# Hybrid decoder layer on one core: other figures in the model of engine times that orders the program, and four gate blocks in place of two ahead of the SSM's drain

## The chip, the cores and the metric

The kernel runs on one core of a Trainium2 chip. The metric is the device time of one execution in microseconds (us), median of several. Engines are named as in the profile: PE (TensorE, matrix multiply), PEld (its weight loads), DVE (VectorE), ACT (ScalarE), POOL (GpSimd) and SP (SyncE, which here only issues transfers). Each works off its own queue of instructions in order and waits on semaphores of the others.

## What is computed

One decoder layer on 512 tokens of width 1024, in float32. Cut to what matters here:

```python
h = rms_norm(x, norm_mix)
qa, ka, va, u, qm, km, vm, gates = split_in(h @ w_in)
oa = swa_attention(qa, ka, va, sinks, slopes)       # window of 128
ys = s5_ssm(u, ...)            # 32 groups: B u, complex scan over time, Re(C h) + D u
z  = gelu(ys) @ w_glu
yb = (z[:, :512] * sigmoid(z[:, 512:])) @ w_o_ssm
om = moba_attention(qm, km, vm, slopes)              # blocks of 256
g  = sigmoid(gates)                                   # 3 x 1024 columns
x  = x + (g0 * (oa @ w_o_swa) + g1 * yb + g2 * (om @ w_o_moba)) @ w_out
x  = x + square(relu(rms_norm(x, norm_ffn) @ w_ff1)) @ w_ff2
out = rms_norm(x, norm_final)
```

## The kernel before, in words

**Dense blocks.** The projections are cut into blocks of 128 output columns. `dense()` computes one: for each of 8 slices of the contraction three matmuls (high part of the weight by high and by low part of the input, low part of the weight by high part), so 24 matmuls of 128x512 into one of two PSUM banks with the tag `acc`. The weights come through `Stream`: SP loads `wraw`, ACT rounds it (`w<-wraw`, CAST) and DVE subtracts for the low part (`w<-wraw,w`); these two are emitted some half blocks ahead of their use. After a block, its bank is emptied: for a gate by one ACT instruction (`gb<-acc`); for a query block `q` by two of ACT and two of DVE (`q<-acc`); for the key block `k` by two chains ACT, ACT, DVE, ACT, one for each half. Block n+2 can't start before block n's bank is empty.

**The plan.** `plan` lists the blocks in order: 4 of the SSM's input `u`, 8 gates of branch 0, SWA's 4 `q`, `k` and `v`, then A gates, the SSM's drain, the start of SWA attention, MoBA's 4 `q`, `k`, `v`, then B gates, SWA's drain, the start of MoBA attention, C gates, and the output projections. Gates of branches 1 and 2 are taken in order from one list, so A, B and C only say where the next ones stand.

**Side work.** The SSM and both attentions are generators, woven between the matmuls of dense blocks: after each slice `dense()` calls `step()`, which lets a side generator emit its next piece when its inputs are ready. "Ready" is not measured: while the program is built, every call of an engine goes through `Engine`, which adds an estimated cost to that engine's clock `clk` and notes when each tile is written. `step()` compares those clocks, and takes nothing more when ACT's or DVE's clock is past the end that is passed in. A `drain` emits what is left of a branch with no dense block between.

```python
def step(end, most=4):
    for _ in range(most):
        if max(clk["ACT"], clk["DVE"]) > end + SLACK:
            return
        x = next((x for x in sides if x.ready() <= clk["PE"] + 0.1), None)
        if x is None:
            return
        x.run()
```

**The SSM's side work.** First `ssm_b`, `ssm_c` and `ssm_phasors` build tables: transposes `pz` evacuated by ACT to `zl`, ACT's pads `ca`, small products `pg`, cosines and sines. Then `ssm_run` treats four groups in two generators, two groups each, one tile `own` for each generator. A group is: products `er`, `ei` on PE (PSUM tag S, three banks); six DVE products and sums and two scans into `own` (called stage 1 below); six more DVE instructions through tiles `p`, `t` into `own` (stage 2); 12 products `y` on PE; then ACT square, two of DVE, ACT tanh and one of DVE into `U`. The drain ends with 16 transfers `yt<-U` on POOL's queue.

**Attention.** A unit has its scores `s` on PE (tag S too), DVE's biased maximum (`p<-s`, `mx`), ACT's exponentials, DVE's scaling, and for each block of keys transposes `pt`, a rounding `th` on ACT, the rest `tl` on DVE, and two products `po`; at the end ACT's `ot` and DVE's `raw` free the one bank of `po` for the next unit.

Of the kernel before, what the change touches and what calls it, by code (L numbers as in the profile page):

```python
# [19 lines left out]
def trunk(ctx: ExitStack, tc: tile.TileContext, x, norm_mix, w_in, sinks, lam_re, lam_im,  # L20
# [3 lines left out]
    clk = dict.fromkeys(("PE", "ACT", "DVE", "POOL", "DMA"), 0.0)  # L24
# [17 lines left out]
    def on_chip(v):  # L42
        return isinstance(v, bass.AP) and not v.tensor.name.startswith(("in_", "out_"))

    def account(eng, outs, ins, cost, after=0.0):
        t = max([clk[eng], ready(*ins) if ins else 0.0])
        for o in outs:
            t = max(t, free_at.get(o.tensor.name, 0.0),
                    max(touched.get(c, 0.0) for c in cells(o)))
        clk[eng] = t + cost  # L50
        for o in outs:
            for c in cells(o):
                written[c] = t + cost + after
        for v in outs + ins:
            for c in cells(v):
                touched[c] = max(touched.get(c, 0.0), t + cost + after)
# [14 lines left out]
    class Engine:  # L71
# [6 lines left out]
        def __getattr__(self, op):  # L78
            f = getattr(self.e, op)

            def call(o, *a, **k):
                outs = [v for v in (o, k.get("accum_out")) if v is not None and on_chip(v)]
                ins = [v for v in list(a) + list(k.values()) if on_chip(v) and
                       v is not k.get("accum_out")]
                n = 1
                for d in o.shape[1:]:
                    n *= d
                if op == "dma_start":
                    account("DMA", outs, ins, max(0.5, n * o.shape[0] * 1.1e-5), 1.5)
                    return f(o, *a, **k)  # L90
                if self.name == "PE":
                    if op == "transpose":
                        cost = 0.109
                    elif a[0].dtype == F32R:
                        cost = max(n, 256) * 4.24e-4
                    else:
                        cost = max(n, 32) * 1.68e-3
                elif self.name == "ACT":
                    aps = sum(on_chip(v) for v in k.values())
                    cost = 0.06 + n * 8.3e-4 + 0.093 * aps  # L100
                elif self.name == "DVE":
                    if op == "tensor_tensor_reduce":
                        outs.append(a[-1])
                        n += 60
                    cost = 0.07 + n * (5.2e-4 if op in ("tensor_scalar", "tensor_copy") else
                                       1.04e-3)
                else:
                    cost = 0.1 + n * 1.75e-3
                account(self.name, outs, ins, cost)
                return f(o, *a, **k)  # L110

            return call

    PE, ACT, DVE, POOL, SP = (Engine(e, n) for e, n in (
        (nc.tensor, "PE"), (nc.scalar, "ACT"), (nc.vector, "DVE"), (nc.gpsimd, "POOL"),
        (nc.sync, "SP")))
# [25 lines left out]
    def PS(tag, name, shape=(128, 512)):  # L142
        b = {"acc": 2, "S": 3, "T": 2, "O": 1}[tag]
        return slot(tag, b, psum.tile(list(shape), F32, tag=tag, name=nm_(name), bufs=b))
# [79 lines left out]
    plan += [("g", 0, m) for m in range(8)]  # L224
    plan += [("q", "swa", m) for m in range(4)] + [("k", "swa"), ("v", "swa")]
    gs_ = [("g", 1, m) for m in range(8)] + [("g", 2, m) for m in range(8)]
    A, B, C, D, E = 2, 8, 2, 1, 1

    def some(n):
        return [gs_.pop(0) for _ in range(min(n, len(gs_)))]  # L230
# [22 lines left out]
    for job in plan:  # L253
        if job[0] in where:
            w, k, c, width = where[job[0]]
# [376 lines left out]
# [8 lines that stand above are left out]
# [5 lines left out]
    def dense(xh, xl, nk=8):  # L645

        acc = PS("acc", "acc")
        for k in range(nk):
            if k % 4 == 0:
                w = ws.take()  # L650
            rh, rl = xh(k), xl(k)
            PE.matmul(acc, w[:, 0, k % 4, :], rh, start=(k == 0), stop=False)
            PE.matmul(acc, w[:, 0, k % 4, :], rl, start=False, stop=False)
            PE.matmul(acc, w[:, 1, k % 4, :], rh, start=False, stop=(k == nk - 1))
            step(clk["PE"] + (nk - 1 - k) * 0.64)
        return acc

    h_h = lambda k: hh[k // 4][:, k % 4, :]
# [194 lines left out]
    def proj_q(b, pair):  # L853
        d = BR[b]
        acc = dense(h_h, h_l)
        g, e = pair // 2, (pair % 2) * 2
        if g not in d["q"]:
            d["q"][g] = B8([128, 4, 512], "q", F32R)
        q = d["q"][g]
        lo, hi = slice(0, 64), slice(64, 128)  # L860
        s0, s1 = (0.125 / slopes[(8 if b == "moba" else 0) + 2 * pair + i] for i in range(2))
        ACT.mul(q[lo, e, :], acc[lo], s0)
        ACT.mul(q[hi, e + 1, :], acc[hi], s1)
        stt(q[hi, e, :], acc[lo], s0, q[lo, e, :].bitcast(F32), MUL, SUB)
        stt(q[lo, e + 1, :], acc[hi], s1, q[hi, e + 1, :].bitcast(F32), MUL, SUB)

    def proj_k(b):
        d = BR[b]
        acc = dense(h_h, h_l)
        K = d["k"] = B8([128, 2, 2, 512], "k", F32R)  # L870
        for g in range(2):
            p, o = slice(64 * g, 64 * g + 64), slice(64 - 64 * g, 128 - 64 * g)
            ACT.copy(K[p, 0, g, :], acc[p])
            ACT.copy(K[o, 0, g, :], acc[p])
            tt(K[p, 1, g, :], acc[p], K[p, 0, g, :].bitcast(F32), SUB)
            ACT.copy(K[o, 1, g, :], K[p, 1, g, :].bitcast(F32))

    def proj_v(b):
        d = BR[b]
        acc = dense(h_h, h_l)  # L880
        vt = B2([128, 512], "vt")
        ACT.copy(vt, acc)
        d["vt"] = vt
# [820 lines left out]
```

## Time and profile before

| | |
|---|---|
| median of 3 runs | 798.91 us (796.45 to 800.1) |
| the profiled execution | 798.28 us, of which the span from the first to the last instruction 796.5 us |
| granted TensorE clock, mean | 0.995 |
| PE busy | 773.5 us, 97% of the span |
| DVE, ACT busy | 589.5 us (74%), 440.7 us (55%) |
| PE in the chain that ended last | 81% of the span |

Busy time of PE holds overlap: matmuls are pipelined, so a record is longer than the distance to the next one. Waits of PE are what the sections below look for. Dense blocks run from the start to about 417 us; behind them the last projection, the two products of the feed-forward part and the final norm follow.

### The profile page before, as it was taken

Reading aid. Unit: us, or ns where it says so; the run is one execution under the profiler, and the core shown is the slowest. Engines: PE = TensorE matmul, PEld = TensorE weight load, DVE = VectorE, ACT = ScalarE, POOL = GpSimd, SP = SyncE. Lnnn points to the kernel's source line nnn. Section 1 sums busy time; section 2 is a strip of 40 time slices with the busy share of each in tenths; the row PEclk is TensorE's granted clock in tenths of the full one; section 3 lists DMA queues with packets and bytes.
Section 4 is the critical chain, followed back from the end, with each engine's and each line's share of the span. In section 5 each row is a group of like instructions: output and inputs, shape, how many; then the busy total and the mean of one; then the engine's idle time right before and its main releaser. Section 6 shows DMA issues by size and latency. Waiting matters only on the chain.

```text
span 796.5 us, 11554 instructions
## 1 busy us (share of the span) xinstructions
PE 773.5 (97%) x4234; PEld 662.5 (83%) x4234; DVE 589.5 (74%) x1176; ACT 440.7 (55%) x848; POOL 92.0 (12%) x140
## 2 busy tenths in 40 slices
PE   7999999989999999999999999999999999999996
PEld 6887778778888887888888888899999888888885
DVE  5885698766796588877575536888888598976774
ACT  7586733464775566653244425666666565655623
POOL 6041020040011222002212132000000000000000
PEclk9999999999999999999999999999999999999998
DMA  9352373253335789429999899733133565555702
GB/s 244 109 155 77 120 205 94 74 125 118 94 112 158 177 214 257 110 85 301 315 348 262 160 205 259 199 110 103 49 86 96 196 241 185 196 175 173 249 1 105
DMA packets 117720, 130.28 MB, mean 164 GB/s; under 512 B 5304, under 2 KB 87264, under 8 KB 117664
## 3 DMA queue, kind: packets, MB, share of 16 engines
q1 hardware_dynamic: 102544, 91.26, 37.3%
q0 software_dynamic: 14928, 38.03, 20.8%
q8 instruction: 33, 0.54, 0.3%
q10 hardware_dynamic: 192, 0.27, 0.1%
q14 instruction: 23, 0.19, 0.1%
HBM read 119.30 MB, written 37.49 MB: 197 GB/s over the span
## 4 chain that ended last, share of the span: by engine, by line
PE 81%; DVE 12%; ACT 3%; issue 2%; DMA 1%; SPq 0%; DVEq 0%; ACTq 0%
PE f L110 40%; PE acc L110 27%; PE xo L110 5%; DVE w L110 4%; DVE own L110 2%; PE s L110 2%; PE po L110 2%; PE pt L110 2%; PE y L110 1%; DVE t L110 1%; DVE pr L110 1%; PE pg L110 1%; DVE p L110 1%; DMA wraw<-in_w_in_dram 1%; ACT k L110 1%
## 5 line engine op out<-in xcount | busy, mean ns | idle before, releaser
L110 PE MATMUL acc<-hh,w 128*128 128x512 f32 (+1 forms) x672 | 215.9, 387 | 3.2 <-DVE k L110 1.9
L110 PEld LDWEIGHTS acc<-hh,w 128*128 128x128 f32 x672 | 124.8, 189 | 27.3 <-issue 3.9
L110 PE MATMUL acc<-hl,w 128*128 128x512 f32 (+1 forms) x336 | 128.5, 382 | 0.9 <-DVE hl L110 0.9
L110 PE MATMUL f<-h2h,f1w 128*128 128x256 f32 (+1 forms) x456 | 102.7, 313 | 0.2 <-ACT h2h L110 0.2
L110 DVE TENSOR_TENSOR w<-wraw,w 128x512 fp32r<-128x512 f32 x112 | 74.6, 685 | 16.3 <-ACT w L110 16.0
L110 PEld LDWEIGHTS f<-h2h,f1w 128*128 128x128 f32 x456 | 76.8, 191 | 5.6 <-ACT h2h L110 0.5
L110 PE MATMUL f<-w2s,s 128*128 128x512 f32 x336 | 79.2, 390 | 0.7 <-DVE w2s L110 0.6
L110 ACT CAST w<-wraw 128x512 fp32r<-128x512 f32 x112 | 67.3, 619 | 17.4 <-PE acc L110 8.6
L110 PEld LDWEIGHTS f<-w2s,s 128*128 128x128 f32 x336 | 62.9, 188 | 14.6 <-DVE w2s L110 1.0
L110 PEld LDWEIGHTS acc<-hl,w 128*128 128x128 f32 x336 | 63.6, 189 | 11.4 <-DVE hl L110 1.3
L110 PE MATMUL f<-h2l,f1w 128*128 128x256 f32 (+1 forms) x228 | 71.4, 313 | 0.3 <-DVE h2l L110 0.3
L110 PE MATMUL f<-xt,f1w 128*128 128x256 f32 x528 | 67.1, 283 | 0.0
L110 PEld LDWEIGHTS f<-xt,f1w 128*128 128x128 f32 x528 | 65.1, 192 | 0.1
L110 PE MATMUL acc<-o,w 128*128 128x512 f32 x192 | 47.8, 394 | 0.0
L110 ACT ACTIVATE act<-act 128x512 f32<-128x512 f32 (+1 forms) x54 | 31.8, 589 | 28.8 <-DVE act L110 27.7
L110 PEld LDWEIGHTS f<-h2l,f1w 128*128 128x128 f32 x228 | 43.5, 191 | 3.0 <-DVE h2l L110 0.5
L90 POOL DMA_DIRECT2D td<-in_w_ff_dram x42 | 36.3, 1078 | 75.6 <-DMA td<-in_w_ff_dram 74.9
L110 ACT CAST w2s<-wq 128x1024 fp32r<-128x1024 f32 x28 | 28.8, 1051 | 27.2 <-PE f L110 12.8
L110 PE MATMUL f<-w2s,av 128*128 128x512 f32 x168 | 42.6, 389 | 0.0
L90 POOL DMA_DIRECT2D g<-gb x23 | 12.8, 555 | 253.1 <-ACT gb L110 248.3
L110 DVE TENSOR_TENSOR f1w<-f1raw,f1w 128x512 fp32r<-128x512 f32 x53 | 35.9, 683 | 7.0 <-ACT f1w L110 7.0
L110 PEld LDWEIGHTS acc<-o,w 128*128 128x128 f32 x192 | 35.3, 188 | 6.8
(223 smaller groups left out, 1446.3 us busy)
## 6 DMA issues: line engine op xcount, KB each, us to landing
td<-in_w_ff_dram POOLq DMA_DIRECT2D x42, 512.0 KB, 9.5
wraw<-in_w_in_dram SPq DMA_DIRECT2D x40, 512.0 KB, 4.0
f1raw<-in_w_ff_dram SPq DMA_DIRECT2D x32, 512.0 KB, 6.3
tq<-td SPq DMA_DIRECT2D x21, 512.0 KB, 5.0
td<-td POOLq DMA_DIRECT2D x14, 512.0 KB, 10.9
wq<-in_w_ff_dram SPq DMA_DIRECT2D x14, 512.0 KB, 4.4
g<-gb POOLq DMA_DIRECT2D x23, 256.0 KB, 3.3
gl<-g SPq DMA_DIRECT2D x23, 256.0 KB, 8.1
```

The source lines that it names most:

```text
L90: return f(o, *a, **k)
L110: return f(o, *a, **k)
```

## The change

Three things are edited, all of them read while the program is built; no instruction's work is changed. (1) The costs in `Engine`: a 128x512 matmul of the rounded type from 0.217 to 0.2267 us, other matmuls from 1.68 to 0.01 + 1.67 ns a column; a scan on DVE counts twice its columns; `tensor_scalar` and `tensor_copy` get 0.13 in place of 0.07 fixed; ACT's per-partition operands given by position are counted at 0.093 each. (2) A from 2 to 4 and B from 8 to 6. (3) The time that `step()` is told a block still has, from 0.64 to 0.68 a slice.

```diff
                     elif a[0].dtype == F32R:
-                        cost = max(n, 256) * 4.24e-4
+                        cost = 0.0134 + max(n, 256) / 2400
                     else:
-                        cost = max(n, 32) * 1.68e-3
+                        cost = 0.01 + max(n, 32) * 1.67e-3
                 elif self.name == "ACT":
-                    aps = sum(on_chip(v) for v in k.values())
-                    cost = 0.06 + n * 8.3e-4 + 0.093 * aps
+                    aps = sum(on_chip(v) for v in ins) - 1
+                    cost = 0.07 + n * 8.4e-4 + 0.093 * (aps + len(outs) - 1)
                 elif self.name == "DVE":
                     if op == "tensor_tensor_reduce":
                         outs.append(a[-1])
                         n += 60
-                    cost = 0.07 + n * (5.2e-4 if op in ("tensor_scalar", "tensor_copy") else
-                                       1.04e-3)
+                    if op == "tensor_tensor_scan":
+                        n *= 2
+                    cost = 0.07 + n * 1.04e-3
+                    if op in ("tensor_scalar", "tensor_copy"):
+                        cost = 0.13 + n * 5.2e-4
...
-    A, B, C, D, E = 2, 8, 2, 1, 1
+    A, B, C, D, E = 4, 6, 2, 1, 1
...
-            step(clk["PE"] + (nk - 1 - k) * 0.64)
+            step(clk["PE"] + (nk - 1 - k) * 0.68)
```

What it moves is seen in the queues; the numbers at the end of the names only tell tiles apart. DVE before, between the scans of the first SSM group (`own_1103`) and stage 1 of the second (`own_1132`):

```order
L110 SCALAR_TENSOR_TENSOR own_1103<-dec_1116,own_1103 128x512 x2
L110 MEMSET own_1132 128x4 x2
L110 MEMSET dec_1145 128x4
L110 TENSOR_TENSOR own_1132<-er_1135,cos_540 128x512
L110 TENSOR_TENSOR t_128_1148<-ei_1136,sin_541 128x512
```

DVE at the same place in the change (the groups' tiles are `own_1139` and `own_1203` here, `acc_1130` is the bank of the first query block):

```order
L113 SCALAR_TENSOR_TENSOR own_1139<-dec_1152,own_1139 128x512 x2
L113 TENSOR_TENSOR w_1131<-wraw_1058,w_1131 128x512
L113 SCALAR_TENSOR_TENSOR q_1189<-acc_1130,q_1189 64x512 x2
L113 TENSOR_TENSOR w_1174<-wraw_1058,w_1174 128x512
L113 MEMSET own_1203 128x4 x2
L113 MEMSET dec_1216 128x4
L113 TENSOR_TENSOR own_1203<-er_1206,cos_543 128x512
```

The two groups, back to back before, have a query block's evacuation and two weight halves between them. On PE the first pair `er`, `ei` moves from the eighth gate of branch 0 into the first query block, the second from 3 matmuls behind the first to 24 behind it.

DVE before, from the scans of the third group to the evacuation of the key block (`k_1456`):

```order
L110 SCALAR_TENSOR_TENSOR own_1103<-dec_1376,own_1103 128x512 x2
L110 TENSOR_TENSOR w_1318<-wraw_1234,w_1318 128x512
L110 SCALAR_TENSOR_TENSOR q_1311<-acc_1317,q_1311 64x512 x2
L110 TENSOR_TENSOR w_1392<-wraw_1234,w_1392 128x512
L110 TENSOR_TENSOR p_170_1430<-own_1103,cos_540 128x512
L110 TENSOR_TENSOR t_168_1428<-own_1103,sin_541 128x512
L110 TENSOR_TENSOR p_171_1431<-own_1103,sin_541 128x512
L110 TENSOR_TENSOR t_169_1429<-own_1103,cos_540 128x512
L110 TENSOR_TENSOR own_1103<-t_168_1428,t_169_1429 128x4x127
L110 TENSOR_TENSOR own_1103<-p_170_1430,p_171_1431 128x4x127
L110 TENSOR_TENSOR w_1413<-wraw_1282,w_1413 128x512
L110 TENSOR_TENSOR k_1456<-acc_1412,k_1456 64x512 x2
```

And in the change (`k_1445`):

```order
L113 SCALAR_TENSOR_TENSOR own_1139<-dec_1417,own_1139 128x512 x2
L113 TENSOR_TENSOR w_1356<-wraw_1262,w_1356 128x512
L113 TENSOR_TENSOR k_1445<-acc_1355,k_1445 64x512 x2
L113 TENSOR_TENSOR w_1430<-wraw_1262,w_1430 128x512
L113 TENSOR_TENSOR w_1456<-wraw_1311,w_1456 128x512
L113 TENSOR_TENSOR w_1473<-wraw_1311,w_1473 128x512
L113 TENSOR_TENSOR p_180_1502<-own_1139,cos_543 128x512
```

Stage 2 of the third group stands behind the key block's evacuation now, and the last query block's is gone from here. On PE the third `er`, `ei` stands before the last 12 matmuls of the key block itself, where before the 24 of the key block and 15 of the last query block followed it.

PE before, at the start of SWA attention, from the first score on (`acc_1661` is MoBA's first query block):

```order
L110 MATMUL s_1681<-k_1456,q_1225 128x256 x4
L110 MATMUL s_1688<-k_1456,q_1225 128x256 x4
L110 MATMUL acc_1661<-hh_167,w_1503 128x512
L110 MATMUL acc_1661<-hl_169,w_1503 128x512
L110 MATMUL acc_1661<-hh_167,w_1503 128x512
L110 MATMUL s_1703<-k_1456,q_1225 128x256 x4
L110 MATMUL s_1710<-k_1456,q_1225 128x256 x4
L110 MATMUL s_1722<-k_1456,q_1225 128x256 x4
L110 MATMUL acc_1661<-hh_167,w_1503 128x512
```

And in the change (`acc_1733` is the same block):

```order
L113 MATMUL s_1753<-k_1445,q_1189 128x256 x4
L113 MATMUL s_1760<-k_1445,q_1189 128x256 x4
L113 MATMUL acc_1733<-hh_167,w_1613 128x512
L113 MATMUL acc_1733<-hl_169,w_1613 128x512
L113 MATMUL acc_1733<-hh_167,w_1613 128x512
L113 MATMUL s_1775<-k_1445,q_1189 128x256 x4
L113 MATMUL s_1782<-k_1445,q_1189 128x256 x4
L113 MATMUL acc_1733<-hh_167,w_1613 128x512
L113 MATMUL acc_1733<-hl_169,w_1613 128x512
L113 MATMUL acc_1733<-hh_167,w_1613 128x512
L113 MATMUL s_1804<-k_1445,q_1189 128x256 x4
L113 MATMUL s_1811<-k_1445,q_1189 128x256 x4
```

Scores come two by two, with three matmuls between. Just ahead of them the last `y` of the SSM stood between the second gate and this block; in the change it stands behind the ninth matmul of the fourth gate, so 15 matmuls of that gate and 3 of the next block follow it. SWA attention has 12 dense blocks up to its drain in place of 14: the order before has its last `po` at the end of the 11th of them and three blocks with nothing between; the change has it at the ninth matmul of the 12th. On POOL two more gate stores stand ahead of the 16 transfers `yt`.

## Rows read from the trace of the kernel before

**Rows 1.** The page, part 1: busy us, share, instructions.
```profile
PE 773.5 (97%) x4234; PEld 662.5 (83%) x4234; DVE 589.5 (74%) x1176; ACT 440.7 (55%) x848; POOL 92.0 (12%) x140
```
**Rows 2.** Who PE waited for: total us, times, longest us.
```profile
PE acc L110 <- DVE k L110: 1.9, 1, 1.9
PE s L110 <- DVE mx L110: 1.9, 1, 1.9
PE ei L110 <- DVE own L110: 1.6, 1, 1.6
...
PE pg L110 <- ACT zl L110: 1.4, 1, 1.4
...
PE y L110 <- DVE own L110: 1.3, 1, 1.3
...
PE acc L110 <- DVE q L110: 0.8, 1, 0.8
...
PE po L110 <- DVE raw L110: 0.4, 1, 0.4
...
PE po L110 <- DVE tl L110: 0.3, 2, 0.2
```
**Rows 3.** By stretch: length, busy PE, PEld, DVE, ACT, POOL (instructions), granted clock, DMA.
```profile
60.00:100.00 40.00, 36.96 (x281) 30.93 (x280) 24.46 (x45) 26.36 (x43) 3.97 (x5) 1.00 0.32 96
165.00:250.00 85.00, 82.93 (x412) 68.37 (x411) 65.51 (x200) 55.49 (x144) 13.40 (x23) 0.98 0.41 112
250.00:267.00 17.00, 17.00 (x76) 14.08 (x75) 5.17 (x10) 5.99 (x12) 3.29 (x5) 1.00 0.67 199
171.00:174.40 3.40, 3.40 (x11) 2.79 (x11) 3.33 (x17) 2.37 (x12) 2.87 (x7) 0.54 0.94 197
```
**Rows 4.** The chain that ended last: start us, us, what.
```profile
119.67 5.36 PE y L110 x48
...
357.73 59.84 PE acc L110 x264
```
**Rows 5.** DVE in order of time: start us, us, instruction [idle before <-releaser].
```profile
93.40 0.68 DVE L110 TENSOR_TENSOR own<-er,cos 128x512 f32<-128x512 f32 x1 [1.85 <-PE ei L110]
...
128.00 0.69 DVE L110 TENSOR_TENSOR own<-er,cos 128x512 f32<-128x512 f32 x1 [0.48 <-PE er L110]
...
133.85 0.67 DVE L110 TENSOR_TENSOR w<-wraw,w 128x512 fp32r<-128x512 f32 x1
...
136.56 0.68 DVE L110 TENSOR_TENSOR p<-own,cos 128x512 f32<-128x512 f32 x1
...
140.29 0.68 DVE L110 TENSOR_TENSOR w<-wraw,w 128x512 fp32r<-128x512 f32 x1
141.00 0.68 DVE L110 TENSOR_TENSOR k<-acc,k 64x512 fp32r<-64x512 f32 x1
```
**Rows 6.** PE in order of time, around waits of rows 2.
```profile
66.88 2.01 PE L110 MATMUL pg<-ca,b 128*32 128x32 f32 x32 [1.41 <-ACT zl L110]
...
90.94 0.38 PE L110 MATMUL er<-U,zl 128*128 128x128 f32 x2
...
92.64 0.48 PE L110 MATMUL acc<-hh,w 128*128 128x512 f32 x1
...
144.40 0.47 PE L110 MATMUL acc<-hh,w 128*128 128x512 f32 x1 [1.92 <-DVE k L110]
...
169.44 1.25 PE L110 MATMUL s<-k,q 128*128 128x256 f32 x8 [1.91 <-DVE mx L110]
...
170.53 0.44 PE L110 MATMUL acc<-hh,w 128*128 128x512 f32 x1
170.77 0.63 PE L110 MATMUL acc<-hl,w 128*128 128x512 f32 x1
```
**Rows 7.** ACT in order of time, ahead of the first pg.
```profile
64.65 1.71 ACT L110 ACTIVATE ca<-w,st 128x256 f32<-128x256 f32 x4
```
**Rows 8.** Instructions that touch po, 160 to 270 us: count, duration, first and last start.
```profile
L110 DVE TENSOR_TENSOR raw<-po,ot x16: 407/417/419, 198.9 to 251.6; 64x256 f32<-64x256 f32 x16
```

## The prediction

> **What bounds the kernel now.** I read the shares of the page first. PE is busy for 97% of the span [rows 1], and where dense blocks stand alone it goes at 59.84 / 264 = 0.2267 us a matmul [rows 4]. The change removes no PE work, so it can only take away waits, or add some. The view of who PE waited for [rows 2] puts a price on that. Between 60 and 180 us, while the SSM is woven in, six waits stand: 1.4 for the first `pg`, 1.6 for the second `ei`, 0.8 for a query block's bank, 1.9 for the key block's bank, 1.3 for the last `y`, 1.9 for attention's scores, together 8.9 us. Behind them the attentions have 0.7 for `po`, and the rest of the list lies in the first 20 us or in the feed-forward part, whose order doesn't move. Five of the six wait for DVE.
>
> One more loss isn't a wait. [...] It fell right behind the wait of 1.9 us that ends at 169.44 [rows 6]; the wait ahead of that one in the program is the 1.3 for `y`. It costs 3.40 x (1 - 0.54) = 1.6 us. So 8.9 + 1.6 = 10.5 us are to be had.
>
> **The units of the walk.** From the rows: a dense block is 24 x 0.2267 = 5.44 us of PE; a group's `er`, `ei` 1.7 (90.94 to 92.64 [rows 6]); its 12 `y` 5.36 / 2 = 2.7 [rows 4]. On DVE stage 1 takes 133.85 - 128.00 = 5.9; weight half, query evacuation and weight half together 136.56 - 133.85 = 2.7, in which a weight half is 141.00 - 140.29 = 0.7 with its hand-over and 0.6 without; stage 2 140.29 - 136.56 = 3.7 [rows 5]. Instructions not shown in the new order are taken at these.
>
> **The first two groups.** Let 0 be the end of the first `er`, `ei` in the new order, in block q0. DVE begins 0.8 later (92.64 [rows 6] to 93.40 [rows 5]). It reaches: end of stage 1 at 6.7; q0's bank free at 8.8; second stage 1 from 9.4 to 15.3; q1's bank free at 17.3; stage 2 of the first group done at 21.6 (weight half 0.6, then 3.7); q2's bank free at 23.6; stage 2 of the second at 27.9; q3's bank at 29.9. PE: rest of q0 4.8, three matmuls 0.7, `er` and `ei` 1.7, rest of q1 4.8, so q2 begins at 12.0 and q0's bank has long been free. q3 begins at 17.4, with q1's bank free at 17.3. The key block k begins at 22.9, and q2's bank comes at 23.6: a wait of **0.7**. Three matmuls and `y` bring it to 27.0, three more to 27.7, and the second `y` needs stage 2 at 27.9: **0.1**, after its first product of 0.1 that needs none of it. So the waits of 1.6 (a fourth bank of tag S asked for while DVE had just begun) and of 0.8 are traded for 0.8. Nothing excludes a zero here, and the upper bound is the 1.6 and 0.8 of before.
>
> **The key block.** `y` ends at 30.5, six matmuls and `er`, `ei` at 33.6. DVE, at 29.9 with a weight half and five short instructions of the two `y` (some 3 us) to do, is ready there. Stage 1 takes it to 39.5, the weight half to 40.1, where the key evacuation starts. Before, 144.40 - 141.00 = 3.4 us lay between that start [rows 5] and the restart of PE [rows 6], two chains ACT, DVE, ACT. So PE restarts at 43.5, while 12 matmuls of k and the 24 of v end at 33.6 + 8.2 = 41.8. The wait is 1.7, less some 0.1 by which a wait in rows is shorter than the distance it makes: **1.6**, against 1.9. What is gained by stage 2 standing behind it is lost because `er` now has 12 matmuls ahead of the key block's end and not 39. Bounds: 0 if DVE's stage 1 comes earlier, 1.9 as before. Queued behind it on DVE are three weight halves; the first is wanted 2.7 us behind PE's restart, so they cost nothing.
>
> **Drain and scores.** From 43.5 one gate and three matmuls take PE to 49.6, where stage 2 of the third group ended at about 49.1. The fourth group's `er` ends near 54; DVE does stage 1, two weight halves, two short ones and stage 2 in some 11.9 us, by 65.9, and the last `y` is asked for at 66.3 (21 + 24 + 9 matmuls on). So the wait of 1.3 goes: **0**, with a margin of 0.4 and the 1.3 as upper bound. The cover is the two gates that stand there now. Behind that `y` 18 matmuls run, 4.1 us, in which DVE and ACT finish the GELU; before, three did. That backlog is why the third pair of scores waited 1.9 for `mx`. Now DVE is at the scores when they come and PE brings them in pairs: **0**, bounded by 1.9.
>
> **The first pg.** Before, it started at 66.88 [rows 6], behind a `zl` copy queued behind the pads `ca`, which end at 64.65 + 1.71 = 66.4 [rows 7]. In the new order that bank is emptied ahead of the pads, so only they hold it. PE would have been there at 66.88 - 1.41 = 65.5; now two pieces `pz` fewer and three matmuls (0.7) more stand ahead of it, which I let cancel. The wait is **1.0**, between 0.5 and 1.4.
>
> **The clock.** With the two waits ahead of it gone I take 0 for the fall at 171; bounds 0 and 1.6. [...]
>
> **Attention.** Two gates leave SWA's stretch. What covers that: between 250 and 267 us PE is busy 17.00 of 17.00 with dense matmuls alone while DVE works 5.17 and ACT 5.99 [rows 3]; 16.3 us of cover are unused, and 10.9 are taken. DVE had 65.5 us of work in the 85 before [rows 3], so on the mean it isn't the bound. I leave `po`'s 0.7 as it is. POOL's transfers of `yt` are wanted only by the second half of the projections of SWA, far behind.
>
> **Sum.** Left are 1.0 + 0.7 + 0.1 + 1.6 = 3.4 of 10.5 us: a gain of 7.1. The profiled execution took 798.28 us, so 791.2; the median of the runs is 798.91, 0.6 above it, inside their own spread.
>
> **The rivals.** *The clock falls anyway.* The waits of 0.7 and 1.6 us lie some 20 us apart with `y` and `er` between, much like the pair that brought it down. Against it: the waits for `pg` and `ei`, 1.4 and 1.6, left it at 1.00 from 60 to 100 us [rows 3]. It adds 1.6: 792.8. *DVE is later than its rows.* Four places above have margins of 0.5 us or less (q3's start, the second `y`, the last `y`, the fourth score). If DVE or ACT is 2 us late in each half of the stretch, PE waits about 2 more in each, as it can't be ahead of DVE for long: 7.1 - 4 = 3.1 gained, 795.2, no change. For it: DVE had little idle time in the walk; against it: the walk counts all that stands in its queue. *Attention runs out of cover*, which would make it slower. The last of SWA's eight units has to end inside 12 blocks. In the stretch before, eight units ended between 198.9 and 251.6 us [rows 8], 52.7 / 7 = 7.5 us a unit with cover, so a unit left without any costs PE at most 7.5: one takes back the gain, two make it 791.2 + 15 = 806. For it: the order has the last `po` only 15 matmuls ahead of the end, so a lag of 3.4 us uses the block up. Against it: the order before needed 11 blocks for the same units and the new one takes 11 and 9 matmuls, so nothing is squeezed; only the spare is gone.
>
> **How the numbers follow.** I give the forecast 0.58, the clock 0.12, the late DVE 0.20, attention 0.10. About 0.5% (4 us) is what a measurement of this kernel can tell from no change, so below 794.9 is faster: 0.58 + 0.12 and a little of the third, 0.71; same 0.20; slower 0.09. The time is 791.2. The low end is all waits of the stretch and of `po` gone, 798.3 - 10.5 - 0.7 = 787; the high end takes in the late DVE with some to spare, 797. Beyond it lie most of the tenth for attention and few of the rest.
>
> **What would show it.** In the list of PE's waits, `ei`, `y` and `mx` should be gone or under 0.5, `k` near 1.6, a `q` near 0.7, `pg` near 1.0; the granted clock 1.00 from 100 to 260 us; in SWA's last blocks no wait for `raw` or `tl` above 0.5. A `k` of 3, a `q` of 2, or waits for `po` of several us would make the prediction wrong, and so would a wait on a transfer, of which the walk has none.

## The result, and the profile after

| | before | after |
|---|---|---|
| median, us | 799.5 (796.45 to 801.64, 4 runs) | 790.87 (790.06 to 791.79, 4 runs) |
| profiled execution, its span | 798.28, 796.5 | 791.46, 789.2 |
| granted TensorE clock, mean | 0.995 | 0.999 |

The ratio is 0.9897, with a 95% interval of 0.9876 to 0.9917: faster by 1%. Here and below, a run over 1.5% above the fastest of its kernel counts in the median but not in the ratio. The span of the profiled execution lost 7.3 us; the forecast was 7.1. Busy time hardly moved, as it should where no instruction's work is changed. Part 1 of the page of the changed kernel, to be held against [rows 1]:

```profile
PE 773.1 (98%) x4234; PEld 662.0 (84%) x4234; DVE 589.2 (75%) x1176; ACT 441.2 (56%) x848; POOL 92.3 (12%) x140
```

Who PE waited for in the changed kernel (total us, times, longest us), against [rows 2]:

```profile
PE acc L113 <- DVE k L113: 1.4, 1, 1.4
...
PE pg L113 <- ACT zl L113: 0.9, 1, 0.9
...
PE acc L113 <- DVE ga L113: 0.5, 2, 0.3
...
PE acc L113 <- DVE q L113: 0.2, 1, 0.2
```

Of the six waits of the SSM's stretch three are gone: `ei`, `y` and `mx` aren't in the list at all. Three are left with 1.4 + 0.9 + 0.2 = 2.5 us in place of 8.9. The entries for `po` are gone, and one of 0.5 for `ga` is new; it stands at 307 and 310 us, in SWA's output projection and in the SSM's `z` product behind it, and no step of the prediction has it.

The windows of the changed kernel (length, busy PE, PEld, DVE, ACT, POOL with instructions, granted clock, DMA), against [rows 3]:

```profile
60.00:100.00 40.00, 39.08 (x286) 32.73 (x285) 22.91 (x41) 29.53 (x50) 6.47 (x9) 1.00 0.40 122
...
165.00:250.00 85.00, 84.86 (x437) 70.49 (x436) 63.99 (x197) 55.46 (x143) 14.68 (x25) 1.00 0.48 130
250.00:267.00 17.00, 17.00 (x91) 14.50 (x90) 11.89 (x45) 10.30 (x29) 3.03 (x4) 1.00 0.72 171
171.00:174.40 3.40, 3.40 (x25) 3.04 (x24) 2.09 (x10) 2.94 (x4) 2.50 (x5) 1.00 0.42 100
```

The last row is the stretch in which the clock had been at 0.54: 11 matmuls are recorded in it before, 25 now, short scores among them, at 1.00. In the third, once dense blocks alone, DVE works 11.89 us in place of 5.17: attention has moved into the spare cover, and PE lost nothing there.

PE of the changed kernel in order of time, at the places of [rows 6]:

```profile
66.84 2.01 PE L113 MATMUL pg<-ca,b 128*32 128x32 f32 x32 [0.86 <-ACT zl L113]
...
98.47 0.48 PE L113 MATMUL acc<-hh,w 128*128 128x512 f32 x1
...
121.81 0.47 PE L113 MATMUL acc<-hh,w 128*128 128x512 f32 x1 [0.20 <-DVE q L113]
...
131.82 0.47 PE L113 MATMUL acc<-hh,w 128*128 128x512 f32 x1
...
141.70 0.47 PE L113 MATMUL acc<-hh,w 128*128 128x512 f32 x1 [1.43 <-DVE k L113]
...
164.67 0.38 PE L113 MATMUL y<-U,tm 128*128 128x128 f32 x2
...
171.80 1.19 PE L113 MATMUL s<-k,q 128*128 128x256 f32 x8
```

The rows at 98.47 and 131.82 are the first dense matmuls behind the first and third `er`, `ei`. The last `y`, at 164.67, and the first scores, at 171.80, have no bracket: PE came there without waiting. DVE of the same execution, against [rows 5]:

```profile
98.53 0.69 DVE L113 TENSOR_TENSOR own<-er,cos 128x512 f32<-128x512 f32 x1 [0.49 <-PE er L113]
...
120.27 1.39 DVE L113 SCALAR_TENSOR_TENSOR q<-acc,q 64x512 fp32r<-64x512 f32 x2
...
131.88 0.69 DVE L113 TENSOR_TENSOR own<-er,cos 128x512 f32<-128x512 f32 x1 [0.16 <-PE er L113]
...
137.73 0.67 DVE L113 TENSOR_TENSOR w<-wraw,w 128x512 fp32r<-128x512 f32 x1
138.31 0.68 DVE L113 TENSOR_TENSOR k<-acc,k 64x512 fp32r<-64x512 f32 x1
...
163.62 0.68 DVE L113 TENSOR_TENSOR own<-p,p 128x508 f32<-128x508 f32 x1
```

The key block reads as forecast: `er` and `ei` end at 131.82, stage 1 takes 131.88 to 137.73, the evacuation begins at 138.31, PE restarts 3.39 us behind that. The last stage 2 ends at 163.62 + 0.68 = 164.30, 0.6 ahead of the product at 164.88 that needs it.

### The profile page after: what moved, and what is told of

Read it like the earlier page. It is cut to its first block, busy times and chain, and to the rows that moved or that the text cites. A ratio compares the mean times of both kernels' runs of the same rounds, so it can differ in the third digit from the quotient of the medians.

```text
span 789.2 us, 11550 instructions
## 1 busy us (share of the span) xinstructions
PE 773.1 (98%) x4234; PEld 662.0 (84%) x4234; DVE 589.2 (75%) x1176; ACT 441.2 (56%) x848; POOL 92.3 (12%) x140
## 4 chain that ended last, share of the span: by engine, by line
PE 83%; DVE 9%; ACT 3%; DMA 3%; issue 1%; SPq 0%; ACTq 0%; DVEq 0%
PE f L113 40%; PE acc L113 28%; PE xo L113 5%; DVE w L113 3%; PE po L113 2%; PE s L113 2%; PE pt L113 2%; DMA wraw<-in_w_in_dram 2%; PE y L113 1%; DVE own L113 1%; DVE pr L113 1%; PE pg L113 1%; ACT zpre L113 1%; DVE t L113 1%; ACT k L113 1%
```

## The experiments

The ratios are to runs of the kernel before on the same chip. The gates alone, the figures alone, eight gates and the first run of the interleaved halves shared one chip; three gates, five gates and the two runs about the scan's figure another; the last four a third.

**The gates alone.** Edit against the kernel before:

```diff
-    A, B, C, D, E = 2, 8, 2, 1, 1
+    A, B, C, D, E = 4, 6, 2, 1, 1
```

> The kernel before with A = 4 and B = 6 alone; the costs and the 0.64 stay. Theory of the prediction: the two gates cover the SSM's drain and nothing else, so PE's waits for y (1.3 us) and mx (1.9 us) go and with them the fall of the clock (1.6 us), while pg 1.4, ei 1.6, q 0.8 and k 1.9 stand as before: 4.8 us off 798.3, so 793.5, a ratio of 0.994. Rival, the figures alone make the gain: the list of PE's waits is that of before, 798, ratio 1.00. Rival, the clock falls at the first scores whatever stands ahead of them: y and mx gone but a granted clock of about 0.54 for 3 us behind the first scores, 795, ratio 0.996.

Measured: 794.87 us, ratio 0.9951 (0.993 to 0.9972). `y` and `mx` are gone from the list of PE's waits, while `k` 1.9, `ei` 1.6, `pg` 1.4 and `q` 0.8 stand as in [rows 2]. From 160 to 180 us, with the first scores, the granted clock was 1.00, but in the profiled execution it fell behind the wait for `k`, where it hadn't before (1.00 from 144 to 148 us there). PE at that place, and a window over it:

```profile
143.43 0.63 PE L110 MATMUL acc<-hh,w 128*128 128x512 f32 x1 [1.90 <-DVE k L110]
143.85 0.63 PE L110 MATMUL acc<-hl,w 128*128 128x512 f32 x1
```
```profile
143.00:146.60 3.60, 3.17 (x12) 2.91 (x13) 2.93 (x5) 2.86 (x5) 0.00 (x0) 0.58 0.46 135
```

So two gates cover the drain and nothing else, as the first theory has it, and here the clock fell behind a single wait: in the 20 us from 120 to 140 PE was busy for 20.00.

**The figures alone.** Edit against the changed kernel:

```diff
-    A, B, C, D, E = 4, 6, 2, 1, 1
+    A, B, C, D, E = 2, 8, 2, 1, 1
```

> The changed kernel with A = 2 and B = 8 put back; the new costs and the 0.68 stay. Theory of the prediction: pg 0.9, q 0.2 and k 1.4 as in the changed kernel and no ei, but the last y stands 12 matmuls (2.7 us) earlier than with four gates and three matmuls ahead of the scores: a wait for y of 1.3 to 2.3 us, one for mx near 1.9, and a granted clock of about 0.54 for some 3 us behind them (1.6): 4.8 to 5.8 us more than 790.9, so 795.7 to 796.7, ratio to before 0.996. Rival, the figures alone make the gain: 791, no wait for y or mx above 0.5. Rival, the fall of the clock needs something other than the two waits: y and mx are there and the clock stays at 1.00, 794 to 795.

Measured: 802.4 us, ratio 1.0051 (1.0031 to 1.007): slower than before, which neither the theory nor a rival had. PE's waits, and a window behind the first of them:

```profile
PE y L113 <- DVE own L113: 6.2, 1, 6.2
PE s L113 <- DVE mx L113: 1.5, 1, 1.5
PE acc L113 <- DVE k L113: 1.4, 1, 1.4
```
```profile
161.70:166.00 4.30, 4.27 (x20) 4.27 (x21) 0.57 (x1) 0.00 (x0) 0.00 (x0) 0.50 0.00 0
```

The expectation had miscounted: the last `y` stands 33 matmuls earlier than with four gates, 9 + 24 of them, or 7.5 us, not 12. By the prediction's own walk it is asked for at 66.3 - 7.5 = 58.8 and ready at 65.9, less 0.6 for one weight half that DVE no longer has ahead of it (the rows stand under the three gates below). That makes a wait of 6.5; it was 6.2. The new figures put the SSM's third and fourth group later, so with two gates more of its chain stands in the drain. That is the point of the whole change:

| ratio to before | costs and 0.64 of before | costs and 0.68 of the change |
|---|---|---|
| A = 2, B = 8 | 1 | 1.0051 |
| A = 4, B = 6 | 0.9951 | 0.9897 |

The figures cost half a per cent with two gates and give as much with four. What each of them does, the scan's apart, no run separates.

**Three gates.** The same line with `3, 7`.

> The changed kernel with A = 3 and B = 7. The last y stands at the end of the third gate, 27 matmuls or 6.1 us behind its place with A = 2, where PE waited 6.2 for it, and three matmuls ahead of SWA's start. Theory, the cover is worth what it is long: y 0.1; behind it the scores come at once, so mx between 0 and the 1.5 it had with A = 2; clock 1.00; 791 to 792.5. Rival, four gates are needed: y above 1.5 and a fall of the clock, 794 or more.

Measured: 795.04 us, ratio 0.9947 (0.9925 to 0.9969). The profiled execution took 798.14, with a wait of 1.3 in the feed-forward part among others. Its two waits ahead of attention:

```profile
PE s L113 <- DVE mx L113: 1.9, 1, 1.9
...
PE y L113 <- DVE own L113: 1.3, 1, 1.3
```

The rival comes nearer, and the sum can be mended: the `y` stands one block of 5.44 us behind its place with two gates, not 6.1, and the third gate puts one more weight half, 0.6, ahead of it on DVE. DVE's weight halves at that place with two, with three and with four gates, and the row of `y` with three:

```profile
156.23 0.67 DVE L113 TENSOR_TENSOR w<-wraw,w 128x512 fp32r<-128x512 f32 x1
...
158.38 1.27 DVE L113 TENSOR_TENSOR w<-wraw,w 128x512 fp32r<-128x512 f32 x2
...
158.24 1.27 DVE L113 TENSOR_TENSOR w<-wraw,w 128x512 fp32r<-128x512 f32 x2
...
164.49 0.71 PE L113 MATMUL y<-own,ca 128*128 128x128 f32 x4 [1.34 <-DVE own L113]
```

The row of `y` with two gates has 6.18. 6.18 - 5.44 + 0.6 = 1.34, and the row says 1.34. The fourth gate moves `y` by 9 matmuls, 2.0 us, and brings no weight half more: 2.0 - 1.3 leaves a margin of 0.7, and 0.6 was measured. So here a gate is worth the length that it puts ahead of `y`, less the weight halves that it brings. Behind `y` only three matmuls stand ahead of the scores, as before the change, and `mx` and the fall of the clock (a mean of 0.91 from 160 to 180 us) come back with them.

**Five gates, and eight.** The same line with `5, 5` and with `8, 2`.

> The changed kernel with A = 5 and B = 5. The SSM's part is that of the change; of SWA's units the last two pt and po of one stand in the drain with nothing between. With A = 8 some four units stood there and the time was 17 us above the change. Theory, only what is uncovered costs: below a unit, 1 to 3 us in waits for tl, th or raw at the end of SWA, 792 to 794. Rival, a wait there costs nothing, since the next dense block follows at once: 791.

> The changed kernel with A = 8 and B = 2: four more gates ahead of the start of SWA attention, 8 dense blocks left up to its drain for its eight units. Theory of the rival in the prediction, attention runs out of cover: four units stand in the drain with nothing between their steps; each costs PE at most the 7.5 us of a covered unit less PE's own work in it, so PE waits for tl, raw, mx and th by 10 to 25 us in all and the time is 801 to 816. Rival, cover is not needed, since PE goes on with MoBA's first scores or DVE keeps up: no wait above 1 us in the drain, 791. The SSM's part is as in the changed kernel in either case: k 1.4, no y, no mx ahead of the drain.

Measured: with five gates 793.19 us, ratio 0.9926 (0.9895 to 0.9957); with eight 808.03, ratio 1.0101 (1.0071 to 1.013). Waits with five:

```profile
PE s L113 <- DVE mx L113: 1.1, 1, 1.1
...
PE po L113 <- DVE tl L113: 0.4, 2, 0.2
```

Waits with eight, and three windows of its drain:

```profile
PE po L113 <- DVE raw L113: 4.9, 4, 1.9
...
PE pt L113 <- DVE p L113: 1.0, 1, 1.0
```
```profile
250.00:255.00 5.00, 3.15 (x12) 2.61 (x13) 4.16 (x17) 3.59 (x12) 0.37 (x1) 0.70 0.79 160
255.00:260.00 5.00, 3.14 (x14) 2.16 (x14) 4.76 (x19) 3.55 (x13) 0.00 (x0) 0.84 0.01 2
260.00:265.00 5.00, 3.94 (x19) 3.08 (x18) 4.91 (x18) 3.14 (x10) 0.00 (x0) 0.78 0.00 0
```

Attention does run out of cover, by degrees. The end of one unit left bare costs 2 to 3 us, 1.1 of it where MoBA's first scores find DVE still busy. Some four bare units cost 16 by the ratios (1.0101 against 0.9897, of 798 us), about 4 each, with DVE at 83 to 98% and the clock between 0.70 and 0.84 beside the waits. Four gates are between two losses: `y` with three, attention with five.

**One figure alone.** Edit against the kernel before (shortened: the scan's lines stand where the change has them, and the cost of `tensor_scalar` and `tensor_copy` is written anew with its old value):

```diff
-                        cost = max(n, 32) * 1.68e-3
+                        cost = 0.01 + max(n, 32) * 1.67e-3
...
+                    if op == "tensor_tensor_scan":
+                        n *= 2
...
-    A, B, C, D, E = 2, 8, 2, 1, 1
+    A, B, C, D, E = 4, 6, 2, 1, 1
```

The first of these lines is a second figure of the change, the cost of the other matmuls. It moves nothing here: the program without it has the same instructions in the same order on every engine. So this run is one of the scan's figure with the four gates.

> The kernel before with two edits of the change alone: a scan on DVE counts twice its columns, and A = 4, B = 6; all other costs and the 0.64 stay. By the queues the first two er, ei stand 24 matmuls apart, in the last gate of branch 0 and the first query block, and the key block's evacuation on DVE stands ahead of the third group's stage 2, with 39 matmuls between that group's er and the end of the key block. Theory, each wait follows from these places: ei gone, q 0.2, k 0 to 0.4 (DVE reaches the key block some 11 us behind er, PE wants its bank 14.3 behind it, and the chains take 3.4), pg 1.4 as before, a second y of 0 to 1.0; with the drain covered as in the run with the gates alone that is 1.6 + 0.6 + 1.5 and the 1.7 of a fall of the clock behind k off 794.9, so 790 to 791.5, level with the whole change. Rival, the other figures carry a part of their own: ei or k stay above 1.0 and the time at 792.5 or more.

Measured: 787.85 us, ratio 0.9871 (0.9837 to 0.9906). The one wait of PE between 60 and 180 us in its list is `pg` with 1.4; `ei`, `k`, `q` and `y` are all gone. That is 2 us below the lower end of what was expected; the change and this kernel stand on one chip further below.

**All but that figure.** Edit against the changed kernel:

```diff
-                    if op == "tensor_tensor_scan":
-                        n *= 2
```

> The changed kernel with a scan on DVE counted once, as before; the other figures, the gates and the 0.68 stay. By the queues the first two er, ei are 3 matmuls apart again, both in the first query block, whose evacuation stands behind both groups' stage 1 on DVE; from the third group on the order is that of the change. Theory: ei 1.6 comes back and with it a q of 0.8 to 2.5, pg 0.9 and k 1.4 as in the change, no y, no mx: 2.2 to 3.9 us more than 790.9, so 793 to 795. Rival, a wait so early is made up for before the drain, PE being held by DVE at the key block in any case: k falls by what ei and q cost, and the time stays at 791 to 792.

Measured: 793.73 us, ratio 0.9934 (0.9915 to 0.9954). The waits:

```profile
PE acc L111 <- DVE q L111: 2.1, 3, 0.8
...
PE ei L111 <- DVE own L111: 0.9, 1, 0.9
...
PE acc L111 <- DVE k L111: 0.8, 1, 0.8
PE y L111 <- DVE own L111: 0.5, 1, 0.5
```

`ei` and the query blocks' banks are back with 0.9 + 2.1 = 3.0, and a `y` with 0.5 that wasn't expected. The rival has a small part of it: `k` falls from 1.4 to 0.8. The scan's cost is what parts the first two groups.

**The key block's halves interleaved.** Edit against the changed kernel, in the key block's evacuation:

```diff
-        for g in range(2):
-            p, o = slice(64 * g, 64 * g + 64), slice(64 - 64 * g, 128 - 64 * g)
+        halves = [(g, slice(64 * g, 64 * g + 64), slice(64 - 64 * g, 128 - 64 * g)) for g in range(2)]
+        for g, p, o in halves:
...
+        for g, p, o in halves:
...
+        for g, p, o in halves:
```

> The changed kernel with the two halves of the key block's evacuation interleaved: ACT's copies of both halves, then DVE's two subtractions, then ACT's two copies back. Theory: PE's wait for k is the two chains one behind the other, 3.4 us from DVE's first subtraction to PE's restart; interleaved they take some 1.5 us less, so the wait of 1.4 falls to 0.3 or less and the time by 1.2 to 1.4 us, to 789.6, ratio to before 0.988. Rival, what holds the bank is that DVE gets to the key block late (stage 1 of the third group stands ahead of it), not the chains: the wait stays above 1.0 and the time at 790.9. Rival, the microsecond gained is lost at the next place where PE catches up with DVE (the last y): k gone, a new wait for y of 0.5 to 1.4 us, 790.9.

Measured: 789.03 us, ratio 0.9888 (0.9865 to 0.9911). The wait for `k` is gone and no `y` in its place. From 100 to 160 us PE is busy for 59.81 us where the change has 58.37:

```profile
100.00:160.00 60.00, 59.81 (x323) 51.34 (x322) 55.71 (x89) 24.00 (x43) 3.88 (x5) 1.00 0.46 120
```

**The three best on one chip, and the kernel before once more.**

> The changed kernel once more, on the chip on which the next two run, so that the three are compared with the same runs of the kernel before: a ratio of 0.990, k 1.4, pg 0.9, q 0.2, clock 1.00 between 60 and 345 us.

> The kernel with the doubled scan cost and the four gates alone, again. Theory: it has no wait for k (1.4 in the change) and a longer one for pg (1.4 against 0.9), so it is 0.9 to 1.5 us faster than the change beside it, a ratio of 0.9885; its earlier 0.987 was partly the chip. Rival, the other figures cost something that the waits don't show: 2 us or more faster than the change beside it.

> The change with the key block's two halves interleaved, again: the wait of 1.4 us for k gone and nothing in its place, so 1.4 us faster than the change beside it, a ratio of 0.988. Rival, the 1.8 us between the two earlier medians were the chips: level with the change, within 0.5 us.

> The kernel before, profiled a second time, for the clock. Theory of the prediction, the clock falls where two waits stand close together (1.3 for y and 1.9 for mx): again a granted clock near 0.54 for some 3 us behind the wait for mx near 169 us and 1.00 behind the wait of 1.9 for k near 144. Rival, a single wait of 1.9 us may or may not bring it down, as the run with the gates alone showed behind k: a fall behind k, behind mx, behind both or behind neither; 796 to 800 with the profile's span longer by some 1.6 for each fall.

Measured: the change 790.03 us, ratio 0.9876 (0.9853 to 0.9899), with its waits of the SSM's stretch as in the first profile; the one figure with the gates 787.79, ratio 0.985 (0.9825 to 0.9876); the interleaved halves 789.51, ratio 0.9883 (0.9856 to 0.9909). The scan's figure and the gates are therefore 2.2 us faster than the whole change, the best kernel here. A window of it shows PE without a pause through the SSM, where the change is busy for 58.3 of the 60 us:

```profile
100.00:160.00 60.00, 60.00 (x332) 52.04 (x331) 54.96 (x89) 23.43 (x42) 4.44 (x6) 1.00 0.51 132
```

Counted from the first 128x512 matmul to the end of the dense blocks, it is 2.4 us ahead of the change: 0.6 behind at `pg`, 2.2 ahead over the query and key blocks, and 0.8 ahead from there on, part of which is `ga`, that it doesn't have. So the rival is right that the other figures cost something of their own: the longer `k`, since they keep the key block's end close behind `er`, and `ga`.

The interleaved halves are 0.5 ahead of the change by the median, where 1.4 was expected; their runs (789.24 to 793.28) and those of the change (789.34 to 790.18) overlap, so the rival, level within 0.5, isn't excluded. Block for block, in the two profiles of this chip, PE is 1.5 us ahead from the key block into SWA attention and 0.6 ahead behind it. So 0.9 is given back inside SWA attention, whose order moved too, in pieces too short for the list of waits; which they are stays open.

The kernel before took 800.82 us in its one run. PE behind its waits for `k` and for `mx`:

```profile
145.47 0.47 PE L110 MATMUL acc<-hh,w 128*128 128x512 f32 x1 [1.93 <-DVE k L110]
145.78 0.39 PE L110 MATMUL acc<-hl,w 128*128 128x512 f32 x1
...
170.54 1.54 PE L110 MATMUL s<-k,q 128*128 128x256 f32 x8 [1.92 <-DVE mx L110]
171.89 0.63 PE L110 MATMUL acc<-hh,w 128*128 128x512 f32 x1
```

Matmuls at 0.39 behind the one, at 0.63 behind the other: the clock fell behind `mx` alone (0.62 from 170.5 to 175 us, 1.00 from 145 to 149), as in the first profile.

## Why the prediction was right

*The sum.* 10.5 to be had and 3.4 left gave 7.1; the span says 7.3. That the two are so close is partly luck. The waits left in the stretch are 2.5 instead of 3.4, and the 0.7 for `po`, left as it was, went too, which makes 10.5 + 0.7 - 2.5 = 8.7. Against that stand `ga` with 0.5 and a wait for a transfer, 2.5 us into the span:

```profile
PE gain L113 <- DMA sg__71<-in_norm_mix_dram: 0.7, 1, 0.7
```

A wait on a transfer was named as a sign of being wrong. This one lies ahead of everything that the change moves, and the second profile of the changed kernel doesn't have it. 8.7 - 0.5 - 0.7 = 7.5; the last 0.2 is not accounted for.

*The first two groups.* `ei` went and the second `y` is not in the list (0.1 was forecast). The `q` wait was 0.2, not 0.7, and one row explains most of it: the walk let DVE begin 0.8 behind `er`, `ei`, taken from a place where it waited for `ei` [rows 5, 6]. Here it began at 98.53 and PE left them at 98.47. With that 0.7 taken off, q2's bank comes at 22.9 in the walk, just as PE does: at 98.5 + 22.9 = 121.4. PE started at 121.81, so the walk thus mended is 0.4 short. At the third pair the walk let DVE begin at once, and it did (131.88 behind 131.82).

*The key block.* 3.39 from the evacuation to the restart against 3.4, and 1.43 against 1.6: the distance was 1.59, and a wait in a row is some 0.16 shorter than that, not 0.1. The interleaved halves show that the two chains, one behind the other, are the wait: it goes with them.

*Drain and scores.* The last stage 2 ended 0.4 ahead of the start of `y` (164.30 and 164.67), as forecast, and `mx` was 0. The runs with two and three gates show that `y` is the gates' doing, as the step says, but the prediction took the whole of the gates' gain for 1.3 + 1.9 + 1.6 as if the figures had no part in it. With the new figures and two gates the wait would have been 6.2.

*The first pg.* 0.9 against 1.0, by the wrong reason. The step says that only the pads hold it. ACT of the changed kernel at that place:

```profile
66.21 0.58 ACT L113 COPY zl<-pz 128x512 f32<-128x512 f32 x1
66.68 1.71 ACT L113 ACTIVATE ca<-w,st 128x256 f32<-128x256 f32 x4
```

The last pads begin at 66.68 and run past the start of `pg` at 66.84; the copy ahead of them ends at 66.79, and that is what PE waited for, as before. The copy has moved ahead of the pads, as the step says, but ACT comes to it only at 66.21, so the wait lost 0.5 and not all of its 1.4. That 0.9 was met is luck (the step's own 66.4 - 65.5 is 0.9 as well). The two effects let cancel, fewer `pz` and three more matmuls, are not tested: PE was there at 66.84 - 0.86 = 65.98, 0.5 later than before, but it had also begun its matmuls behind the last `x` 0.5 later (at 18.60 and not 18.05).

*The clock.* It stayed at 1.00 from 60 to 345 us, as taken. The 1.6 that the sum counts for the fall is an estimate, the length of the stretch by the share of the clock that was missing in it [rows 3]. The cause given, two waits close together, was not needed: with the gates alone it fell behind a single wait of 1.90. What the runs show is that the wait of 1.9 for `mx`, behind which it had fallen, went, and that it stayed at 1.00 behind the waits left (1.4, 0.9 and 0.2).

*Attention.* The rival didn't come, with four gates. That it is real, and that it starts at five, is shown; its price of up to 7.5 us a unit was an upper bound, and about 4 was measured.

## What to carry to other kernels

Figures of a model that orders a program, and the work that is put there as cover, have to be tried together: the cover alone took 0.5% off, the figures alone added 0.5%, both took 1.0% off. Then try the figures one by one, since one of them, the scan's, held the gain of the figures and the others took some of it back (2.2 us on one chip). And price cover by its length less what it brings to the engine that is waited for.

## What was not expected of the hardware

In these profiles the length of a wait doesn't settle whether the granted clock falls behind it. Of six waits of 1.90 to 1.93 us, in the two profiles of the kernel before, the run with the gates alone and that with three gates, it fell behind four: the three for `mx` and one of the three for `k`. That one is of the run with the gates alone, whose PE order up to there is that of the kernel before, where the other two passed without a fall. The falls in the second profile of the kernel before and with three gates:

```profile
170.50:175.00 4.50, 4.46 (x18) 4.05 (x19) 4.01 (x22) 2.78 (x14) 3.97 (x9) 0.62 0.97 230
...
172.00:177.00 5.00, 4.63 (x19) 4.17 (x20) 4.44 (x25) 3.01 (x15) 4.49 (x9) 0.66 0.94 219
```

The four short falls cost an estimated 1.5 to 1.7 us each, worked out from their windows as length by (1 - clock), and behind the wait of 6.2 the granted clock was 0.50 for 4.3 us. Behind `pg` (1.4), `ei` (1.6), the `mx` of 1.5 with the figures alone and the `k` of the changed kernel and of its runs with other gates (1.4 to 1.5, six profiles) it never fell: it is 1.00 in each window over them. Nor is a fall seen behind two longer waits in the feed-forward part: 2.4 with eight gates, where the mean from 420 to 800 us is 1.00, and 2.20 in the second run of the interleaved halves, where the mean of the whole profile is 0.999 and the two matmuls behind the wait take 0.72 us:

```profile
503.06 0.72 PE L113 MATMUL f<-h2h,f1w 128*128 128x512 f32 x2 [2.20 <-DVE f1w L113]
```

The falls seem to come and go between executions of one kernel: of the thirteen of the kernel before on the chip of the gates alone, three had a mean granted clock of 0.999 and spans of 794.2 to 794.6 us, the other ten 0.993 to 0.997 and 796.1 to 799.8. Which stretches fell there no trace shows, and what tells a wait with a fall behind it from one without stays open.
